# Rotary queries of layer 1: projected among the gates and kept in DRAM, instead of inside the attention

## The chip, the cores and the metric

The kernel runs on one core of one Trainium2 chip. The metric is device time in microseconds from launch to end; one execution was also taken by the hardware profiler. The engines are TensorE (PE, with its weight loads PEld), VectorE (DVE), ScalarE (ACT), GpSimd (POOL) and SyncE (SP), which issues the DMAs here.

## The reference, cut to what matters

Two layers run over 256 context tokens and 1024 latent tokens. Layer 0 is differential attention. Layer 1 is multi-head latent attention, and the change is in it:

```
proj = h @ w_in                      # -> q_a (384), kv_a (256), k_pe (64), gate (1024)
q = (rmsnorm(q_a, g_qa) @ w_qb)      # 8 heads x (128 nope + 64 rope)
q_pe = apply_rope(q[..., 128:])      # latent tokens alone; halves x1, x2 of 32:
                                     # [x1*cos - x2*sin, x1*sin + x2*cos]
s = q . [k_nope, k_pe] * 192**-0.5   # per head, 1280 keys for latents, 256 for context
o = softmax(s) @ v;  out = o * silu(gate)
```

So each of 8 heads has 128 query columns without position (qn) and 64 rotary ones (qpe); the rotary key is shared by the heads.

## The kernel before, in words

All matrix products are made in three terms of a high and a low part (`mm3`, L328 to L330: high x high, high x low, low x high), so each operand exists twice. Tokens go in 5 pairs of 128-row blocks (`NPAIR`): 4 pairs of latents, 1 pair of context.

Layer 1 has two stages that matter here. **First the projections and gates** (`l1_items`): three token items give the compressed keys, the rotary key and the compressed queries, whose normalised transposes are `m.qaT[pr]`, high and low. Then come eight `gate_item(h)`, one per head: 24 matmuls of 512 columns twice and 24 of 256 columns, into PSUM buffers of a pool of four (`pj`), each result put through a tanh on ScalarE and a product on VectorE and stored in DRAM (`gTd`). `chain` runs the items in turn; an item's `yield None` is the point at which the next item's weights are loaded, through staging buffers `wst`, of which there are three.

**Then the attention** (`l1_heads`): 8 heads x 10 blocks of queries ("units"). The order is written by hand: in turn n the scores of unit n + 2 (`l1_scores`), the values of the pair just finished (`l1_values`), the transposes of unit n, and between them "fills", generators that make the next heads' operands: `l1_kn` ("k"), `l1_qn` ("q"), `l1_v` ("v", two heads at a time, for even heads) and `l1_qpe` ("p", four heads at a time). Which fill stands where comes from `DA`, `DB`, `DC` (the start), `at(...)` and the tables `QO`, `QE`, `KS`, `VS`, `PS`. "p" of heads 0 to 3 is made in head 0, "p" of heads 4 to 7 over heads 3 and 4. Within each engine a scheduler sets the final order.

`l1_qpe` makes, for each pair, 18 matmuls with the tokens as rows, copies the result out, rotates it (six operations of 128 columns for a block, one block on VectorE, one on GpSimd; `rope_inplace`), splits it into high and low, transposes it with 8 transposes (L1219) and copies the two PSUM tiles out (L1221). The result has a head's high and low rotary columns on the 128 partitions, and the rotary part of the scores is then two matmuls, against `kpA` and `kpB`.

`weights_x` is what layer 0 uses to load weights with the two rotary halves apart: 32 first-half columns of four heads together, then the 32 second-half columns. The products made with it are transposed, and rotating them needs no shuffling inside a row.

Of the kernel before, what the change touches and what calls it, by code (L numbers as in the profile page):

```python
# [81 lines left out]
class K:  # L82
# [265 lines left out]
    def weights_x(self, W, off):  # L348


        nc, wp = self.nc, self.wp
        out = []
        for k0 in range(0, KC, 2):
            wh = self.t(wp, [P, 2, 2, P], "wh", F32R)
            wl = self.t(wp, [P, 2, 2, P], "wl", F32R)
            st = self.t(wp, [P, 2, 256], "wst", bufs=3)
            nc.sync.dma_start(st, W[:, k0:k0 + 2, off:off + 256])
# [4 lines left out]
            out += [(wh[:, :, j, :], wl[:, :, j, :]) for j in range(2)]  # L362
        return out
# [6 lines left out]
    def l0_qk_item(self, kind, hp):  # L370
# [90 lines left out]
        return lambda: self.weights_x(W, (0 if kind == "q" else 1024) + hp * 256), gen  # L461
# [742 lines left out]
    def l1_qpe(self, h, out):  # L1204

        nc, c, m, I = self.nc, self.c, self.m, self.I
        Wq = I["mla_w_qb"][0].rearrange("(kc p) n -> p kc n", p=P)
        wq = self.weights(Wq, [((h + j) * 192 + P, 64) for j in range(4)], lo_engs=self.LO[::-1] if h == 0 else None)
        yield 1
        res = out["p", h] = []  # L1210
        pend = []

        def finish(pr, qss):
            o = self.t(c.qp, [P, 4, 256], f"qpe{pr}", F32R)
            res.append(o)
            for i in range(2):
                pt = self.t(c.tp, [P, 4, P], "tp")
                for j in range(4):
                    nc.tensor.transpose(pt[:, j, :].bitcast(F32R), qss[i][:, j].rearrange("p a d -> p (a d)"),  # L1219
                                        self.identr)  # L1220
                (nc.scalar.copy if i else nc.vector.tensor_copy)(o[:, :, i * P:(i + 1) * P], pt)  # L1221
        for pr in range(NPAIR):
            ps = self.l1_ps("p")
            qt = m.qaT[pr]
            for i in range(2):
                for k in range(3):
                    self.mm3(ps[:, i, :], (qt[:, 0, k, i * P:(i + 1) * P], qt[:, 1, k, i * P:(i + 1) * P]),
                             wq[k], k == 0, k == 2)
            qss = []
            for i in range(2):  # L1230
                raw = self.t(c.rp, [P, 4, 64], "qraw", bufs=2)
                nc.scalar.copy(raw.rearrange("p a d -> p (a d)"), ps[:, i, :])
                if pr < CTXP:
                    self.rope_inplace(c.rp, raw.unsqueeze(1), 2 * pr + i, 4, nc.gpsimd if i else nc.vector, bufs=2)
                qs = self.t(c.rp, [P, 4, 2, 64], "qs", F32R, bufs=2)
                nc.vector.tensor_copy(qs[:, :, 0, :], raw)
                nc.vector.tensor_tensor(out=qs[:, :, 1, :], in0=raw, in1=f32(qs[:, :, 0, :]), op=ALU.subtract)
                qss.append(qs)
            yield 1960
            finish(pr, qss)  # L1240
            yield 470

    def l1_scores(self, u, kn, qn, qpe):
# [7 lines left out]
        qp = qpe[u.pr][:, u.h % 4, u.i * P:(u.i + 1) * P]  # L1251
# [63 lines left out]
    def l1_heads(self):  # L1315
# [78 lines left out]
    def run(self, ctx):  # L1394
# [339 lines left out]
```

## Time and profile before

| | |
|---|---|
| median of 3 runs | 2013.87 us (2013.73 to 2016.31) |
| the profiled execution, its own time | 2013.29 us |
| its span | 2011.5 us |
| gates (from 1210 us to their end at 1324.2 us) | 114.2 us |
| head 0 of the attention, with its start | 107.7 us |
| heads 1 and 2; 3 and 4; 5 and 6 | 128.2; 148.7; 129.9 us |
| DMA: q1, the SyncE queue | 222.70 MB, 35.4% of 16 engines' span |

The span runs from the first to the last instruction. A head is taken to end where the last product with its gate (L1302) starts. The busy time of an engine is the union of its instructions; the idle time of a stage is its length less that. A matmul's own duration is longer than the step to the next one, because they overlap, so prices per matmul are taken from the steps between starts.

### The profile page before, as it was taken

What the parts mean: (1) busy time and instruction counts of PE and PEld (TensorE: products, weight loads), DVE (VectorE), ACT (ScalarE), POOL (GpSimd) and SP (SyncE); (2) the same over time, 40 slices, a digit from 0 to 9 for tenths busy, and PEclk for the clock granted to TensorE, in tenths of its full rate; (3) what the DMA queues carried; (4) which work ended last, traced back from release to release, by engine and by line L of the source; (5) the groups of instructions that cost most, each with busy time, mean ns of one, the idle gap of its engine ahead of it and who ended that gap; (6) DMA issues with size and microseconds to landing.
All of it is one profiled execution on the core that took longest, in us unless ns stands there. A gap on an engine that the chain in (4) does not pass through costs nothing. (4 is left out here: it accounts for less than half of the span.)

```text
span 2011.5 us, 36299 instructions
## 1 busy us (share of the span) xinstructions
PE 1921.2 (96%) x13548; PEld 1729.7 (86%) x13548; DVE 1257.4 (63%) x2518; ACT 966.0 (48%) x2421; POOL 522.1 (26%) x740
## 2 busy tenths in 40 slices
PE   6999999999999999999989899999999999999998
PEld 5788888798988878887988898888999899998998
DVE  4634347788878777888246623157776877777413
ACT  4422124667666666677335533234444444455421
POOL 3355442213122212324243431011000110003214
PEclk9999999999999999999999999999999999999999
DMA  8545544454355453456343302210101011013412
GB/s 304 186 160 185 179 144 144 145 156 141 111 168 180 116 171 101 139 158 207 128 135 112 101 24 85 76 38 26 31 29 34 16 31 34 27 38 95 154 60 105
DMA packets 215536, 225.07 MB, mean 112 GB/s; under 512 B 24032, under 2 KB 184128, under 8 KB 215232
## 3 DMA queue, kind: packets, MB, share of 16 engines
q1 hardware_dynamic: 215200, 222.70, 35.4%
q8 instruction: 107, 1.75, 0.4%
q14 instruction: 69, 0.57, 0.1%
q10 hardware_dynamic: 160, 0.05, 0.0%
HBM read 153.14 MB, written 69.53 MB: 111 GB/s over the span
## 5 line engine op out<-in xcount | busy, mean ns | idle before, releaser
L328 PE MATMUL pj<-wh,hh 128*128 128x256 f32 (+1 forms) x1264 | 369.9, 293 | 6.6 <-DVE ptl L670 3.5
L329 PE MATMUL pj<-wl,hh 128*128 128x256 f32 (+1 forms) x1264 | 359.5, 284 | 6.0 <-DVE wl L321 3.7
L330 PE MATMUL pj<-wh,hl 128*128 128x256 f32 (+1 forms) x1264 | 359.2, 284 | 3.4 <-POOL hl L300 1.5
L321 POOL TENSOR_TENSOR wl<-wst,wh 128x512 fp32r<-128x512 f32 (+3 forms) x98 | 113.5, 1165 | 577.8 <-ACT wh L320 487.8
L328 PEld LDWEIGHTS pj<-wh,hh 128*128 128x128 f32 x1264 | 242.4, 192 | 11.6 <-DVE ptl L670 4.1
L329 PEld LDWEIGHTS pj<-wl,hh 128*128 128x128 f32 x1264 | 242.6, 192 | 8.3 <-DVE wl L321 4.1
L330 PEld LDWEIGHTS pj<-wh,hl 128*128 128x128 f32 x1264 | 242.0, 191 | 6.4 <-POOL hl L300 3.1
L330 PE MATMUL pj<-hh,wl 128*128 128x512 f32 (+1 forms) x512 | 188.5, 368 | 0.2
L328 PE MATMUL pj<-hh,wh 128*128 128x512 f32 (+1 forms) x512 | 188.3, 368 | 0.0
L329 PE MATMUL pj<-hl,wh 128*128 128x512 f32 (+1 forms) x512 | 187.8, 367 | 0.0
L601 DVE TENSOR_REDUCE mA<-S 128x1 f32<-128x1024 f32 x128 | 155.3, 1219 | 46.5 <-PE S L599 45.5
L613 ACT ACTIVATE e<-S,bias 128x1024 f32<-128x1024 f32 x128 | 142.9, 1117 | 81.4 <-DVE bias L610 81.4
L599 PE MATMUL S<-kl,q 128*128 128x512 f32 x512 | 149.1, 411 | 5.7 <-ACT e L613 5.3
L669 ACT CAST pth<-tp 128x512 fp32r<-128x512 f32 (+1 forms) x208 | 99.5, 512 | 83.1 <-PE tp L667 81.9
L669 ACT CAST pth<-pj 128x512 fp32r<-128x512 f32 (+1 forms) x192 | 98.4, 519 | 71.6 <-PE pj L667 68.8
L670 DVE TENSOR_TENSOR ptl<-tp,pth 128x512 fp32r<-128x512 f32 (+1 forms) x208 | 116.0, 580 | 15.1 <-ACT pth L669 14.3
L644 DVE SCALAR_TENSOR_TENSOR e<-e,cf,e 128x512 f32<-128x512 f32 (+1 forms) x192 | 122.5, 680 | 1.1
L670 DVE TENSOR_TENSOR ptl<-pj,pth 128x512 fp32r<-128x512 f32 (+1 forms) x192 | 112.9, 592 | 9.6 <-ACT pth L669 9.1
L320 ACT CAST wh<-wst 128x512 fp32r<-128x512 f32 (+3 forms) x140 | 78.8, 573 | 75.3 <-issue 22.0
L330 PEld LDWEIGHTS pj<-hh,wl 128*128 128x128 f32 x512 | 96.3, 188 | 20.0 <-POOL wl L361 3.0
L329 PEld LDWEIGHTS pj<-hl,wh 128*128 128x128 f32 x512 | 96.3, 188 | 16.9
L328 PEld LDWEIGHTS pj<-hh,wh 128*128 128x128 f32 x512 | 96.3, 188 | 16.4
(333 smaller groups left out, 5296.2 us busy)
## 6 DMA issues: line engine op xcount, KB each, us to landing
q<-qsd SPq DMA_DIRECT2D x320, 64.0 KB, 2.1
wst<-in_da_w_in_dram SPq DMA_DIRECT2D x64, 256.0 KB, 3.1
kl<-ksd SPq DMA_DIRECT2D x64, 192.0 KB, 3.6
wst<-in_w_out_dram SPq DMA_DIRECT2D x48, 256.0 KB, 3.0
ast<-in_w_ada_dram SPq DMA_DIRECT2D x8, 1024.0 KB, 6.4
wh<-in_w_ada_dram SPq DMA_DIRECT2D x32, 256.0 KB, 4.2
wl<-in_w_ada_dram SPq DMA_DIRECT2D x32, 256.0 KB, 5.0
vdh<-s SPq DMA_DIRECT2D x24, 256.0 KB, 2.1
```

What stands on the lines that cost most here:

```text
L320: nc.scalar.copy(wh, st)
L321: (lo_engs or [nc.gpsimd])[k0 // kb % len(lo_engs or [0])].tensor_tensor(out=wl, in0=st, in1=f32(wh), op=ALU.subtract)
L328: nc.tensor.matmul(out, a[0], b[0], start=first, stop=False)
L329: nc.tensor.matmul(out, a[0], b[1], start=False, stop=False)
L330: nc.tensor.matmul(out, a[1], b[0], start=False, stop=last)
L599: nc.tensor.matmul(S[:, so:so + 512], st(cc, o), kl[cc][:, so:so + 512], start=(o == 0), stop=(o == 1))
L601: nc.vector.reduce_max(out=mA[:, cc:cc + 1], in_=S, axis=AX.X)
L613: nc.scalar.activation(u.es[cc][:, 0:1024], A[cc], AF.Exp, bias=bias[:, cc:cc + 1], scale=0.125, accum_out=u.zA[:, cc:cc + 1])
L644: nc.vector.scalar_tensor_tensor(out=w[:, sl], in0=w[:, sl], scalar=cf, in1=e0[:, sl], op0=ALU.mult, op1=ALU.add)
L669: nc.scalar.copy(hi, tp[:, 0:cn, :])
L670: nc.vector.tensor_tensor(out=u.ptl[g][:, 0:cn, u.i * P:(u.i + 1) * P], in0=tp[:, 0:cn, :], in1=f32(hi), op=ALU.subtract)
```

## The change

The rotary queries leave the attention. Two new items `qpe_item(0)` and `qpe_item(1)` stand among the gates, behind gate 1 and behind gate 4, each for four heads. An item loads its weights with `weights_x` (now with a list of columns), and for each pair makes the 18 matmuls with the weights as the stationary side, so that the result is transposed: 128 partitions are 4 heads x 32 columns of one half, and the two halves lie side by side. The rotation of a latent pair is a ScalarE copy, two products of 512 columns with a table loaded from DRAM, a subtraction and an addition of 256 columns on VectorE; then a ScalarE cast gives the high part and VectorE the low part. Four stores put them into DRAM (`qpd`). In the attention `l1_load_p(h)` loads a head's 4 x 32 rows of 1280 columns, head 0's at the start and head h + 1's in turn 3 of head h. `l1_qpe`, its pool and its fills are gone; the pool of the loaded queries has two buffers. The transposes, two per block of four heads before, are gone with it.

```diff
-    DA, DB, DC = "kpqv", "kpqkkpp", "pvvv"
+    DA, DB, DC = "kqv", "kqkk", "vvv"
...
-    PS = (0, 1, 2, 3, 4, 5, 7, 10, 12, 13, 15)
...
-            later.add(self.split_T(tp, "tp", [qa[:, 0, :], qa[:, 1, :]], m.qaT[pr], 3), 12)
+            later.add(self.split_T(tp, "tp", [qa[:, 0, :], qa[:, 1, :]], m.qaT[pr], 3), 12, ("qa", pr))
...
+        def qpe_item(g):
...
+                for pr in range(NPAIR):
+                    if pr < CTXP:
+                        rt = table(pr)
+                    later.finish(("qa", pr))
+                    ps = self.t(pj, [P, 2, 256], "pj")
+                    qt = m.qaT[pr]
+                    for x in range(2):
+                        for k in range(3):
+                            self.mm3(ps[:, x, :], (ws[k][0][:, x, :], ws[k][1][:, x, :]), (qt[:, 0, k, :], qt[:, 1, k, :]),
+                                     k == 0, k == 2)
+                            yield 1
+                    hi, lo = (tile(1 + 2 * (pr % 2) + v, F32R) for v in range(2))
+                    r = ps
+                    if pr < CTXP:
+                        cos, sin = (rt[:, j, :].unsqueeze(1).to_broadcast([P, 2, 256]) for j in range(2))
+                        r = tile(0)
+                        t = self.t(c2.pool, [P, 2, 256], "gTh")
+                        nc.scalar.copy(r, ps)
+                        nc.vector.tensor_tensor(out=t, in0=r, in1=sin, op=ALU.mult)
+                        nc.vector.tensor_tensor(out=r, in0=r, in1=cos, op=ALU.mult)
+                        nc.vector.tensor_tensor(out=r[:, 0, :], in0=r[:, 0, :], in1=t[:, 1, :], op=ALU.subtract)
+                        nc.vector.tensor_tensor(out=r[:, 1, :], in0=r[:, 1, :], in1=t[:, 0, :], op=ALU.add)
+                    nc.scalar.copy(hi, r)
+                    nc.vector.tensor_tensor(out=lo, in0=r, in1=f32(hi), op=ALU.subtract)
+                    for j, v in enumerate((hi, lo)):
+                        for x in range(2):
+                            nc.sync.dma_start(self.qpd[g][2 * j + x][:, pr * 256:(pr + 1) * 256], f32(v)[:, x, :])
+            return lambda: self.weights_x(Wq, [((4 * g + j) * 192 + P, 64) for j in range(4)]), gen
...
+                self.l1_tok_item([(0, 256)], pj, ev_q1, lambda pr: None)] + gates[0:2] + [qpe_item(0)] + gates[2:5] + [
+                qpe_item(1)] + gates[5:] + [(self.l1_first, lambda ws: iter(()))]
...
+    def l1_load_p(self, h):
+
+        q = self.t(self.c.qp, [P, 1280], "qpe", F32R)
+        for b in range(4):
+            self.nc.sync.dma_start(f32(q)[32 * b:32 * b + 32, :], self.qpd[h // 4][b][h % 4 * 32:h % 4 * 32 + 32, :])
+        return q
...
-        at(0, 0, ("p", 0), ("v", 0), ("q", 0), ("v", 0))
-        at(0, 1, ("p", 0), ("v", 0), ("p", 0))
-        at(0, 2, ("q", 0), ("p", 0))
-        at(0, 3, ("v", 0), ("p", 0))
-        at(0, 4, ("p", 0))
+        at(0, 0, ("v", 0), ("q", 0), ("v", 0))
+        at(0, 1, ("v", 0))
+        at(0, 2, ("q", 0))
+        out["p", 0] = self.l1_load_p(0)
...
+            if n % 10 == 3 and h + 1 < H:
+                out["p", h + 1] = self.l1_load_p(h + 1)
```

Three places show how the order on the engines moves. The first is VectorE in the gates, behind the gate of head 1. Before, gate follows gate (`gT` is a gate's tanh, `gTh` its half, `wl` the low part of a weight):

```order
L1123 SCALAR_TENSOR_TENSOR gT_15415<-gT_15415,gTh_15416 128x512
L321 TENSOR_TENSOR wl_15460<-wst_15461,wh_15459 128x512
L1123 SCALAR_TENSOR_TENSOR gT_15447<-gT_15447,gTh_15448 128x256
L1123 SCALAR_TENSOR_TENSOR gT_15490<-gT_15490,gTh_15491 128x512
L1123 SCALAR_TENSOR_TENSOR gT_15522<-gT_15522,gTh_15523 128x512
```

After, the rotation stands between two gates. `qa` are the buffers of the raw, high and low queries, `wst` holds the table, `gTh` the product with the sine:

```order
L320 TENSOR_TENSOR wl_15474<-wst_15475,wh_15473 128x512
L1127 SCALAR_TENSOR_TENSOR gT_15461<-gT_15461,gTh_15462 128x256
L1164 TENSOR_TENSOR gTh_15503<-qa_3139_15502,wst_15479 128x512
L1165 TENSOR_TENSOR qa_3139_15502<-qa_3139_15502,wst_15479 128x512
L1166 TENSOR_TENSOR qa_3139_15502<-qa_3139_15502,gTh_15503 128x256
L1167 TENSOR_TENSOR qa_3139_15502<-qa_3139_15502,gTh_15503 128x256
L1169 TENSOR_TENSOR qa_3138_15501<-qa_3139_15502,qa_3137_15500 128x512
L1164 TENSOR_TENSOR gTh_15539<-qa_3145_15538,wst_15515 128x512
```

Five operations for each latent pair come in here. On ScalarE of the same place the fifth pair's cast (`qa_3160`) comes to stand behind the copies of the other pairs, two casts of gate weights (`wh`) and a gate's tanh:

```order
L1163 COPY qa_3157_15610<-pj_15589 128x512
L319 CAST wh_15656<-wst_15658 128x512
L319 CAST wh_15757<-wst_15759 128x512
L1125 ACTIVATE gT_15687<-pj_15662 128x512
L1168 CAST qa_3160_15642<-pj_15623 128x512
L1168 CAST qa_3155_15608<-qa_3157_15610 128x512
```

The PSUM buffer of the fifth pair (`pj_15623`) is read late in this row. The second place is the SyncE queue where the gates end and the attention starts. Before, behind the last stores of the gates (`gTd`):

```order
L1125 DMA gTd_3_59_118<-gT_16088 128x256
L318 DMA wst_17015<-in_mla_w_qb_dram 128x2x128
L318 DMA wst_17021<-in_mla_w_qb_dram 128x128
L1125 DMA gTd_4_60_119<-gT_16120 128x256
L1294 DMA gTl_16780<-gTd_0_21_80 128x256
```

After:

```order
L1129 DMA gTd_3_59_118<-gT_16456 128x256
L317 DMA wst_17174<-in_mla_w_kvb_dram 128x2x128
L1257 DMA qpe_16531<-qpd_0_61_120 32x1280
L1129 DMA gTd_4_60_119<-gT_16488 128x256
L1257 DMA qpe_16531<-qpd_1_62_121 32x1280
L1257 DMA qpe_16531<-qpd_2_63_122 32x1280
L1257 DMA qpe_16531<-qpd_3_64_123 32x1280
L1311 DMA gTl_16939<-gTd_0_21_80 128x256
```

Three of the four loads of head 0's rotary queries stand behind the last gate's store. The third place is VectorE in head 3, where a piece of a rotation stood among the softmax steps before (`mm`, `bias`, `Z`, `rz`: maxima, sums and their reciprocals; `qs` the split queries):

```order
L345 TENSOR_TENSOR qraw_19183<-qraw_19183,rt_19185 128x4x32
L1236 CAST qs_19192<-qraw_19183 128x4x64
L1236 CAST qs_19204<-qraw_19195 128x4x64
L1237 TENSOR_TENSOR qs_19192<-qraw_19183,qs_19192 128x4x64
L1282 TENSOR_TENSOR Z_19137<-Z_19137 128x1
L1237 TENSOR_TENSOR qs_19204<-qraw_19195,qs_19204 128x4x64
L1284 RECIPROCAL rz_19161<-Z_19137 128x1
```

After, the same softmax steps without it:

```order
L1293 TENSOR_SCALAR bias_19237<-mm_19236 128x1
L674 TENSOR_TENSOR ptl_3823_19213<-tp_19272,pth_3820_19210 128x4x128
L1287 TENSOR_REDUCE mm_19286<-S_19289 128x1
L1299 TENSOR_TENSOR Z_19238<-Z_19238 128x1
L1289 TENSOR_REDUCE mm_19286<-tp_19285 128x1
L1301 RECIPROCAL rz_19262<-Z_19238 128x1
```

The sum `Z` and its reciprocal follow the maxima, with no rotary row ahead of them.

## Rows read from the trace of the kernel before

**Rows 1.** The page's table of busy time, share of the span, instructions.

```profile
PE 1921.2 (96%) x13548; PEld 1729.7 (86%) x13548; DVE 1257.4 (63%) x2518; ACT 966.0 (48%) x2421; POOL 522.1 (26%) x740
```

**Rows 2.** Busy time by stage: gates; head 0; heads 1-2; 3-4; 5-6.

```profile
core 0: us, PE busy (x) PEld busy (x) DVE busy (x) ACT busy (x) POOL busy (x), PEclk, DMA share, GB/s
1210.00:1324.20 114.20, 114.11 (x592) 96.33 (x591) 28.50 (x39) 34.20 (x72) 11.45 (x12) 1.00 0.28 80
1324.20:1431.94 107.74, 102.84 (x756) 94.52 (x755) 76.30 (x185) 49.34 (x121) 18.31 (x33) 1.00 0.11 30
1431.94:1560.11 128.17, 127.32 (x914) 116.85 (x914) 91.81 (x216) 64.11 (x155) 5.45 (x7) 1.00 0.10 29
1560.11:1708.79 148.68, 144.04 (x1048) 131.26 (x1047) 111.09 (x267) 71.14 (x172) 20.37 (x33) 1.00 0.09 28
1708.79:1838.67 129.88, 128.15 (x917) 117.19 (x917) 94.80 (x221) 68.70 (x167) 12.83 (x15) 1.00 0.15 49
```

**Rows 3.** Timeline of VectorE: start, duration; last products of heads 0, 2, 4, 6.

```profile
1431.94 0.40 DVE L1302 TENSOR_TENSOR yT<-tp,gTl 128x256 f32<-128x256 f32 x1
...
1560.11 0.42 DVE L1302 TENSOR_TENSOR yT<-tp,gTl 128x256 f32<-128x256 f32 x1
...
1708.79 0.41 DVE L1302 TENSOR_TENSOR yT<-tp,gTl 128x256 f32<-128x256 f32 x1
...
1838.67 0.42 DVE L1302 TENSOR_TENSOR yT<-tp,gTl 128x256 f32<-128x256 f32 x1 [0.26 <-PE tp L667]
```

**Rows 4.** Chain of waits in head 0: start, time on the chain.

```profile
1380.43 0.63 PE tp L1219 x8
```

**Rows 5.** Timeline of TensorE: gate matmuls of 512, of 256; rotary matmuls in the attention.

```profile
1212.34 0.39 PE L328 MATMUL pj<-hh,wh 128*128 128x512 f32 x1
...
1212.80 0.40 PE L330 MATMUL pj<-hh,wl 128*128 128x512 f32 x1
...
1321.73 0.28 PE L328 MATMUL pj<-hh,wh 128*128 128x256 f32 x1
...
1324.10 0.28 PE L330 MATMUL pj<-hh,wl 128*128 128x256 f32 x1
...
1327.76 0.28 PE L328 MATMUL tp<-qaT,wh 128*128 128x256 f32 x1
...
1329.77 0.28 PE L330 MATMUL tp<-qaT,wl 128*128 128x256 f32 x1
```

**Rows 6.** Timeline of VectorE, ScalarE and GpSimd in the first gates.

```profile
1213.17 0.62 DVE L1036 SCALAR_TENSOR_TENSOR qa<-qa,rs,gq 128x384 f32<-128x384 f32 x1 [0.95 <-POOL rs L254]
...
1214.44 1.29 POOL L321 TENSOR_TENSOR wl<-wst,wh 128x512 fp32r<-128x512 f32 x1
...
1214.51 1.64 DVE L1036 SCALAR_TENSOR_TENSOR qa<-qa,rs,gq 128x384 f32<-128x384 f32 x1 [0.38 <-POOL rs L254]
...
1216.79 0.59 ACT L1025 CAST qaT<-tp 128x512 fp32r<-128x512 f32 x1 [3.28 <-PE tp L1023]
1217.40 0.69 DVE L1026 TENSOR_TENSOR qaT<-tp,qaT 128x512 fp32r<-128x512 f32 x1 [1.26 <-ACT qaT L1025]
...
1218.37 0.42 DVE L1026 TENSOR_TENSOR qaT<-tp,qaT 128x256 fp32r<-128x256 f32 x1 [0.27 <-ACT qaT L1025]
```

**Rows 7.** Line 424, a rotary product of layer 0: ns minimum/median/maximum, first and last start.

```profile
L424 DVE TENSOR_TENSOR r<-r,ropeT x16: 691/691/694, 89.0 to 278.1; 128x512 f32<-128x512 f32 x16
```

**Rows 8.** Timeline of the SyncE queue at the end of the gates.

```profile
1324.30 1.20 SPq L318 DMA_DIRECT2D wst<-in_mla_w_qb_dram  x2
1325.64 0.33 SPq L1125 DMA_DIRECT2D gTd<-gT  x1
```

**Rows 9.** DMA issues by name: count, KB each, median us to landing.

```profile
kl<-ksd SPq DMA_DIRECT2D x64, 192.0 KB, 3.6
...
wst<-in_mla_w_in_dram SPq DMA_DIRECT2D x24, 256.0 KB, 2.8
```

**Rows 10.** Groups by line: count, busy us, mean ns of one, idle before, releasers.

```profile
L1219 PE MATMUL tp<-identr,qs 128*128 128x128 f32 x80 | 9.2, 250 | 2.1 <-DVE qs L1237 0.9 <-DVE qn L1178 0.9 <-DVE knl L1159 0.2
```

More of the change, by code (lines that the diff above doesn't have):

```diff
@@ L346, in rope_inplace, with weights_x @@
         eng.tensor_tensor(out=x2, in0=x2, in1=b[:, 1], op=ALU.add)
-    def weights_x(self, W, off):
+    def weights_x(self, W, cols):
         nc, wp = self.nc, self.wp
+        nk = W.shape[1]
         out = []
[L353 to L357, printed above, removed]
+        for k0 in range(0, nk, 2):
+            kn = min(2, nk - k0)
+            wh = self.t(wp, [P, 2, kn, P], "wh", F32R)
+            wl = self.t(wp, [P, 2, kn, P], "wl", F32R)
+            st = self.t(wp, [P, kn, 256], "wst", bufs=3)
+            o = 0
+            for off, w in cols:
+                nc.sync.dma_start(st[:, :, o:o + w], W[:, k0:k0 + kn, off:off + w])
+                o += w
             sv = st.rearrange("p k (g x d) -> p (k g) x d", g=4, x=2)
@@ L361, in weights_x @@
             nc.gpsimd.tensor_tensor(out=vl, in0=sv, in1=f32(vh), op=ALU.subtract)
-            out += [(wh[:, :, j, :], wl[:, :, j, :]) for j in range(2)]
+            out += [(wh[:, :, j, :], wl[:, :, j, :]) for j in range(kn)]
         return out
@@ L460, in gen @@
                 yield 360
-        return lambda: self.weights_x(W, (0 if kind == "q" else 1024) + hp * 256), gen
+        return lambda: self.weights_x(W, [((0 if kind == "q" else 1024) + hp * 256, 256)]), gen
     def l0_tok_item(self, kind, hp, each=None):
@@ L1126, in gate_item, with gen, table @@
             return lambda: self.weights(W, [(704 + h * P, P)], kb=4, lo_engs=self.LO), gen
+        Wq = I["mla_w_qb"][0].rearrange("(kc p) n -> p kc n", p=P)
+        def qpe_item(g):
+            def gen(ws):
+                yield None
+                tile = lambda j, dt=F32: self.t(c2.pool, [P, 2, 384], f"qa{j}", dt).rearrange("p a b -> p (a b)")[
+                    :, 0:512].rearrange("p (a b) -> p a b", a=2)
+                def table(pr):
+                    rt = self.t(self.wp, [P, 2, 256], "wst", bufs=3)
+                    nc.sync.dma_start(rt, I["ropeT"][:, :, pr * 256:(pr + 1) * 256])
+                    return rt
+                for pr in range(NPAIR):
[26 more added lines that the diff above has]
+            return lambda: self.weights_x(Wq, [((4 * g + j) * 192 + P, 64) for j in range(4)]), gen
@@ L1128, in l1_items @@
+        gates = [gate_item(h) for h in range(H)]
         return [self.l1_tok_item([(384, 256)], pj, ev_kva, lambda pr: later.finish(("h", pr))),
                 self.l1_tok_item([(256, 128), (640, 64)], pj, ev_q2, lambda pr: None),
-                self.l1_tok_item([(0, 256)], pj, ev_q1, lambda pr: None)] + [gate_item(h) for h in range(H)] + [(self.l1_first, lambda ws: iter(()))]
+                self.l1_tok_item([(0, 256)], pj, ev_q1, lambda pr: None)] + gates[0:2] + [qpe_item(0)] + gates[2:5] + [
+                qpe_item(1)] + gates[5:] + [(self.l1_first, lambda ws: iter(()))]
@@ L1202, in l1_v @@
             yield 1310
[L1204 to L1241, printed above, removed]
+    def l1_load_p(self, h):
[3 more added lines that the diff above has]
+        return q
     def l1_scores(self, u, kn, qn, qpe):
@@ L1250, in l1_scores @@
         qh, ql = qn[u.pr][:, 0, u.i * P:(u.i + 1) * P], qn[u.pr][:, 1, u.i * P:(u.i + 1) * P]
-        qp = qpe[u.pr][:, u.h % 4, u.i * P:(u.i + 1) * P]
+        qp = qpe[:, u.pr * 256 + u.i * P:u.pr * 256 + (u.i + 1) * P]
         e = self.t(c.ep, [P, 1280], "e")
@@ L1305, in l1_gen @@
     def l1_gen(self, kind, h):
-        return {"k": self.l1_kn, "q": self.l1_qn, "v": self.l1_v, "p": self.l1_qpe}[kind](h, self.out)
+        return {"k": self.l1_kn, "q": self.l1_qn, "v": self.l1_v}[kind](h, self.out)
     def l1_first(self):
@@ L1328, in scores @@
                 u = units[n]
-                self.l1_scores(u, out["k", u.h], out["q", u.h], out["p", u.h - u.h % 4])
+                self.l1_scores(u, out["k", u.h], out["q", u.h], out["p", u.h])
         fills = {n: [] for n in range(len(units) + 2)}
@@ L1345, in l1_heads @@
                     at(h, max(j, 0 if h else 4), (kind, g))
-        for j in self.PS:
-            at(3, j, ("p", 4))
         for it in self.DB:
@@ L1354, in l1_heads @@
         scores(1)
-        self.pd = "pq"
+        self.pd = "q"
         for n, u in enumerate(units):
@@ L1404, in run @@
         self.gTd = [[self.t(dp, [P, 256], f"gTd{h}_{p}") for p in range(NPAIR)] for h in range(H)]
+        self.qpd = [[self.t(dp, [P, 1280], f"qpd{g}_{b}") for b in range(4)] for g in range(2)]
         self.yTd = [[self.t(dp, [P, 256], f"yTd{h}_{p}") for p in range(NPAIR)] for h in range(H)]
@@ L1639, in run @@
             c.qn = pool(s1, "qn")
-            c.qp = pool(s1, "qp1")
+            c.qp = pool(s1, "qp1", 2)
             c.vp = pool(s1, "vp1")
@@ L1644, in run @@
             c.st = pool(s1, "st1", 2)
-            c.rp = pool(s1, "rp1", 1)
             c.pj = pool(s1, "pj4", self.DP, space=PSUM)
@@ L1648, in run @@
             c.tp, c.ttag = pool(s1, "tps1", self.DT, space=PSUM), "tp"
-            self.pd = "kqvp"
+            self.pd = "kqv"
             self.l1_heads()
```

## The prediction

> **What bounds the kernel now.** I read the page's busy table first [rows 1]. The reader is to see that TensorE is busy for 96% of the span, but this share is an average, so the next view is the one that asks what each stage waits for: busy time by stage, cut at the two places that the change touches and at the ends of heads [rows 2]. In the 114.2 us of the gates TensorE idles 0.1 us: each matmul put there costs its full time, and each wait of another engine there is free as long as it stays shorter than the work in front of it. In the attention TensorE idles 4.9 us in head 0 (107.74 less 102.84), 0.9 us in heads 1 and 2 together, 4.6 us in heads 3 and 4, 1.7 us in heads 5 and 6. Heads 0, 3 and 4 are those that make rotary queries (four heads' worth in head 0, the other four spread over heads 3 and 4), and the VectorE column rises with them: 111.1 us against 91.8 and 94.8 us for the pairs of heads beside them. So the rotary queries cost matmul time, and beyond it waits on VectorE.
>
> The third view gives this a price without any model: the time at which the last product of a head leaves [rows 3]. Heads 1 and 2 take 1560.11 - 1431.94 = 128.17 us, heads 3 and 4 take 148.68 us, heads 5 and 6 take 129.88 us. Each pair holds one odd and one even head with the same fills, except for the rotary queries of heads 4 to 7, and the matmul counts of [rows 2] differ by 131 to 134 where the rotary step has 130. So that step costs 148.68 - 129.03 = 19.65 us where it stands (18.8 to 20.5 by either neighbour).
>
> **The change part by part.**
>
> *Products.* Both kernels make 2 groups x 5 pairs x 18 = 180 matmuls of 256 columns. In the attention 18 of them start over 2.01 us, 0.118 us each; in the last gate 21 start over 2.37 us, 0.1185 us each [rows 5]. Out of the attention go 180 x 0.118 = 21.3 us, into the gates come 21.3 us, which nothing there can hide. Net: nothing.
>
> *Transposes.* 80 transposes of the split queries fall away. In the chain of waits eight of them take 0.63 us, 0.079 us each [rows 4]: 80 x 0.079 = 6.3 us, 3.15 us a group, all on the engine that sets the end.
>
> *Waits in heads 3 and 4.* Of the 19.65 us, 90 x 0.118 = 10.6 us only moves, which leaves 9.0 us (8.2 to 9.9) as gain. 3.15 us of it are transposes; the other 5.9 us are waits, and the cause is the 16 to 19 us of VectorE work (rotation, splitting, copying out) that goes with the step. What is late next there is TensorE itself, as in heads 1 and 2.
>
> *Head 0.* It has no sibling to subtract. The transposes give 3.15 us. Its idle time is 4.9 us against 0.4 us for an ordinary head; some of that is the start of the attention, where nothing is in flight yet. In heads 3 and 4 an extra idle time of about 3.4 us went with 5.9 us of wait, so the waits here lie between 0 (all of it is the start) and 4.5 x 5.9 / 3.4 = 7.8 us. I take 4.0, near the middle, since VectorE also has the rotary work here. Head 0: 7.15 us, between 3.15 and 11.
>
> *The rotation among the gates.* Per pair of context blocks it is now a ScalarE copy, four VectorE operations (two of 512, two of 256 columns), a ScalarE cast and a VectorE subtraction. By the nearest rows [rows 6, 7]: 0.59 + 2 x 0.69 + 2 x 0.42 + 0.59 + 0.69 = 4.1 us, about 4.2 us with the handing over, and the pairs follow each other, because they share one buffer for the raw queries. TensorE makes a pair in 18 x 0.118 = 2.1 us, so the rotation falls behind, and what matters is when the four PSUM buffers come free. The first that can hurt is that of the fifth pair, wanted again by the second gate after the step: 10.6 us for the step and 48 x 0.23 + 24 x 0.118 = 13.9 us for the gate in between [rows 5], that is 24.5 us after the step began. On ScalarE the fifth pair's cast stands behind four raw copies, three of the casts, a gate's tanh and the cast of a gate's weights that are loaded into the buffer of the fourth pair's table. Adding up: 2.1 + 3 x 4.2 + 0.6 = 15.3 us to the fourth copy, then 2.5 us of VectorE work up to the last reader of that table, 2.8 us for the load [rows 9], three ScalarE operations and the subtraction, 2.5 us: about 23.2 us. It just fits, with 1.3 us to spare, so the cost lies between 0 and, with a load twice as slow, 2 x 1.5 us. I take 1 us for both groups and 4 us as the bad end.
>
> GpSimd is the risk in this. Next to a 1.29 us subtraction on GpSimd a VectorE operation with two SBUF inputs took 1.64 us instead of 0.62 us [rows 6]. The Trainium skill, "GPSIMD Engine Reference", section "1. Specifications", says that its SBUF interfaces are shared with VectorE and contend with instructions that have two SBUF inputs, which all five VectorE steps of a pair are. By that rule alone each of them would be open to it; by the rows only those that fall beside one of the two such subtractions of an item, which adds 1 to 2 us and uses up about the spare time. It is the second rival below.
>
> *Queues.* The SyncE queue gets 40 stores, 8 table loads and 32 loads of 160 KB. The loads of heads 1 to 7 are issued a head ahead and are hidden by the whole head. Head 0's cannot be early: three of its four parts stand in the queue behind the last gate's store, which waits for VectorE. From the end of the gates (1324.10 + 0.12, [rows 5]) that store issues after 1.4 us [rows 8]; three issues of up to 0.6 us and 3.6 us until a load of like shape lands [rows 8, 9] make 7.2 us. TensorE first reads it behind 79 matmuls of 256, 4 of 512 and 3 of 256 columns, 10.6 us after the gates. Cost 0; were that cover gone, up to 3.6 us. The rotary weights are cast by the same engines as before, only earlier: 0.
>
> **Sum.** -9.0 (heads 3, 4) - 7.15 (head 0) + 1 (gates) = -15.15 us. Against the profiled execution (2013.29 us, its span 2011.5) that is 1998.1; the median of the runs shown is 0.6 us higher, so 1998.7, which I round to 1999. The ends: -9.9 - 11 = -20.9 us gives 1993, -8.2 - 3.15 + 4 = -7.4 us gives 2006.
>
> **Rivals.** *A, the waits come back.* VectorE was late because of the softmax steps, and without the 180 matmuls there is less to fill TensorE while it waits. Then only the transposes are gained: -6.3 + 1, 2008.5. For it: the chain of a head is long, and part of the idle time in head 0 is the start. Against it: heads 1, 2, 5, 6 have no such matmuls and idle less, not more.
>
> *B, slower: the rotation holds up the gates.* The place is the fifth pair's PSUM buffer. Each microsecond that a pair's chain grows arrives there four times, in each of two groups, less the 1.3 us to spare. The gain is used up, and the 0.2% with it, from (15.15 + 1 + 4) / 2 = 10 us a group, (10 + 1.3) / 4 = 2.8 us a pair, 7.0 instead of 4.2 us. If every VectorE step of a pair were slowed as the one row shows, by 1.0 us, the chain is 9.2 us and the loss 2 x (4 x 5 - 1.3) = 37 us: 2036. For it: the rows of contention. Against it: GpSimd works only 11.5 of the 114.2 us of the gates [rows 2].
>
> *C, the queries arrive late in head 0*, as priced above: 2002. For it: a SyncE queue that serves in order. Against it: 3.4 us to spare.
>
> *D, a transpose holds TensorE for all of its duration.* One lasts 0.250 us in the mean [rows 10]; 80 x (0.250 - 0.079) = 13.7 us more gain, 1985. Against it stands the chain, where eight took 0.63 us. The Trainium skill, "TensorE: Matmul & The Clock Gate", section "Part 4: PE-mode transpose", gives about 275 ns for one inside a kernel, an estimate of 80 x 0.275 = 22 us where the sum has 6.3; the trace agrees with it as a duration and not as a rate.
>
> **How the numbers follow.** Forecast 0.66; A 0.17 (a third of it gains under 4 us); B 0.09 (slower 0.05, no difference 0.03, faster 0.01); C 0.07; D 0.01. About 0.2%, 4 us, is what a measurement of this kernel can tell from no change. Faster: 0.66 + 0.07 + 0.01 + 0.12 + 0.01 = 0.87; same 0.05 + 0.03 = 0.08; slower 0.05. The range 1993 to 2008 leaves out most of B, half of A, D, and the forecast's own low end: about 0.2.
>
> **What the profile will show.** Right: the gates about 136 us long with TensorE idle under 2 us; heads 3 and 4 at 128 to 130 us with VectorE near 93 us and TensorE idle under 2 us; head 0 near 90 us (107.7 - 10.6 - 7.2); no wait for the loaded queries. Wrong: TensorE waiting in the gates for the cast or the subtraction of the fifth pair (B), a wait for the load of the queries at the head of the attention (C), or heads 3 and 4 that idle longer than heads 1 and 2 (A).

## The result, and the profile after

The changed kernel takes 1996.67 us in the median (1993.42 to 1997.65, 5 runs) against 2013.87 us before: a ratio of 0.9909, 95% interval [0.9896, 0.9922], or 18.3 us less (15.7 to 20.9). I had forecast 1999.0 us, 14.9 us less. The profiled execution took 1997.65 us, its span 1995.8 us. The page's busy table, to be held against [rows 1]:

```profile
PE 1911.7 (96%) x13468; PEld 1721.9 (86%) x13468; DVE 1248.4 (63%) x2461; ACT 963.9 (48%) x2409; POOL 498.9 (25%) x693
```

Exactly 80 matmul instructions are gone, the transposes. The shares have not moved, though the kernel is faster: they are averages, as in the view before. What moved is seen by stage. The busy time of each engine in the gates, head 0, heads 1-2, 3-4, 5-6 and 7 of the changed kernel, the answer to [rows 2]:

```profile
core 0: us, PE busy (x) PEld busy (x) DVE busy (x) ACT busy (x) POOL busy (x), PEclk, DMA share, GB/s
1214.31:1349.09 134.78, 134.69 (x767) 116.89 (x765) 53.62 (x81) 46.21 (x93) 14.92 (x16) 1.00 0.42 127
1349.09:1438.82 89.73, 87.78 (x626) 79.89 (x625) 59.56 (x136) 42.62 (x104) 5.85 (x8) 1.00 0.19 54
1438.82:1566.27 127.45, 126.97 (x914) 116.83 (x914) 91.50 (x215) 63.89 (x155) 5.56 (x7) 1.00 0.14 39
1566.27:1694.03 127.76, 127.12 (x916) 116.99 (x915) 91.59 (x217) 63.78 (x155) 5.55 (x7) 1.00 0.14 40
1694.03:1823.89 129.86, 128.06 (x919) 117.31 (x918) 94.82 (x222) 68.25 (x167) 12.79 (x15) 1.00 0.18 54
1823.89:1874.24 50.35, 45.70 (x321) 40.20 (x320) 34.95 (x79) 26.82 (x67) 11.59 (x15) 1.00 0.22 66
```

The gates are read here from their first matmul (1214.31 us), not from a round time as in [rows 2]. The same cut of the kernel before has these two rows, for the gates and for head 7:

```profile
1210.72:1324.21 113.49, 113.40 (x586) 95.62 (x585) 28.21 (x39) 33.48 (x71) 10.73 (x12) 1.00 0.28 80
...
1838.67:1889.96 51.29, 46.69 (x321) 41.53 (x321) 35.48 (x78) 26.76 (x67) 11.51 (x15) 0.97 0.22 65
```

| stage | before, us | after, us | moved | forecast |
|---|---|---|---|---|
| gates | 113.5 | 134.8 | +21.3 | +22.3 |
| head 0 | 107.7 | 89.7 | -18.0 | -17.75 |
| heads 1, 2 | 128.2 | 127.5 | -0.7 | 0 |
| heads 3, 4 | 148.7 | 127.8 | -20.9 | -19.65 |
| heads 5, 6 | 129.9 | 129.9 | 0.0 | 0 |
| head 7 | 51.3 | 50.4 | -0.9 | 0 |
| sum | 679.2 | 659.9 | -19.3 | -15.1 |

The rows show three things. TensorE idles 0.1 us in the gates, as before: the rotation, 25 us more of VectorE, is hidden entirely. Heads 3 and 4 now have the length, the matmul count and the VectorE time of heads 1 and 2: they have become an ordinary pair. And the work ahead of the gates, which the change does not touch, ended at 1210.72 us in the profile of before and at 1214.31 us in that of after. In the ten further profiles below it ended between 1209.7 and 1214.0 us, with either form of the kernel, so this difference of 3.6 us is scatter of single executions; it is why the spans differ by 15.7 us and the stages by 19.3.

### The profile page after: what moved, and what is told of

Read it like the earlier page. It is cut to its first block, busy times and chain, and to the rows that moved or that the text cites. A ratio compares the mean times of both kernels' runs of the same rounds, so it can differ in the third digit from the quotient of the medians.

```text
span 1995.8 us, 36154 instructions
## 1 busy us (share of the span) xinstructions
PE 1911.7 (96%) x13468; PEld 1721.9 (86%) x13468; DVE 1248.4 (63%) x2461; ACT 963.9 (48%) x2409; POOL 498.9 (25%) x693
## 4 chain that ended last, share of the span: by engine, by line
PE 43%; DVE 5%; POOL 3%; ACT 2%; issue 2%; DMA 2%; SPq 0%; POOLq 0%; ACTq 0%; DVEq 0%
PE pj L327 7%; PE pj L329 7%; PE pj L328 7%; PE tp L671 3%; PE tp L327 3%; PE tp L328 3%; PE tp L329 3%; PE S L1280 1%; PE S L1281 1%; PE S L1278 1%; PE S L1279 1%; PE S L1277 1%; PE S L603 1%; DVE ptl L674 1%; DMA yst<-yTd 1%
## 5 line engine op out<-in xcount | busy, mean ns | idle before, releaser
L329 PEld LDWEIGHTS pj<-hh,wl 128*128 128x128 f32 x512 | 96.3, 188 | 20.9 <-POOL wl L365 3.9
L603 PEld LDWEIGHTS S<-kl,q 128*128 128x128 f32 x512 | 88.8, 192 | 25.1 <-ACT e L617 8.1
```

Source lines behind the costliest of these rows:

```text
L329: nc.tensor.matmul(out, a[1], b[0], start=False, stop=last)
L603: nc.tensor.matmul(S[:, so:so + 512], st(cc, o), kl[cc][:, so:so + 512], start=(o == 0), stop=(o == 1))
```

## The experiments

The sum came out right, but it rested on a split that no row showed: 3.15 us of transposes and 5.9 us of waits in heads 3 and 4. My theory (theory 1 below) was that the waits are VectorE's load, and that the transposes' time comes on top. The rival (theory 2) was that the transposes, queued on TensorE behind the splitting, are what waits.

**Without the rotation.**

```diff
-                if pr < CTXP:
-                    self.rope_inplace(c.rp, raw.unsqueeze(1), 2 * pr + i, 4, nc.gpsimd if i else nc.vector, bufs=2)
```

> The kernel before, with the rotation of the rotary queries left out (they stay unrotated); the matmuls, the splitting, the transposes and the copies stay. Theory 1, the waits in heads 0, 3 and 4 come from VectorE's own load: its work in heads 3 and 4 falls by about a third of the 17.8 us that the step has there, so heads 3 and 4 fall from 148.7 us to 143 to 147 us, head 0 from 107.7 to 105 to 107 us, the time by 3 to 8 us to 2006 to 2011 us. Theory 2, the waits come from the transposes, which stand in TensorE's queue behind the splitting: the rotation is only a part of the chain ahead of them, heads 3 and 4 stay within 1.5 us of 148.7 and the time within 3 us of 2013.9.

Head 0 and heads 3 and 4 of this kernel, same columns as above:

```profile
1327.26:1429.25 101.99, 101.70 (x756) 94.30 (x755) 68.45 (x160) 49.26 (x121) 6.64 (x9) 1.00 0.11 31
1557.40:1701.44 144.04, 142.85 (x1048) 131.16 (x1047) 102.14 (x242) 70.49 (x172) 7.41 (x9) 1.00 0.10 28
```

Head 0 loses 5.7 us, heads 3 and 4 lose 4.6 us; the ratio to before is 0.994 [0.9918, 0.9963]. The transposes all still stand (1048 matmuls, as before) and TensorE idles 1.2 us instead of 4.6 us. What TensorE waits for in heads 3 and 4 of the kernel before (who waits, for whom: us in total, times, longest):

```profile
PE tp L328 <- DVE ptl L670: 2.9, 3, 1.5
PE tp L1260 <- DVE ptl L670: 1.2, 1, 1.2
```

Here `ptl` are the low parts of the probabilities, a softmax step on VectorE. None of the waits there ends with the split queries that the transposes (L1219) read, and without the rotation this is the longest one left:

```profile
PE tp L1219 <- DVE qpe L1221: 0.8, 1, 0.8
```

So theory 2, which had heads 3 and 4 within 1.5 us of 148.7, falls for them; in head 0 the transposes do wait, for 2.1 of its 4.9 us of idle time [rows 10]. Head 0 gave a little more than theory 1 allowed, and so did the time, 2004.93 us where 2006 to 2011 was expected.

**Without the transposes.** Copies from SBUF take the place of the copies from PSUM. It ran twice:

```diff
-                pt = self.t(c.tp, [P, 4, P], "tp")
-                for j in range(4):
-                    nc.tensor.transpose(pt[:, j, :].bitcast(F32R), qss[i][:, j].rearrange("p a d -> p (a d)"),
-                                        self.identr)
-                (nc.scalar.copy if i else nc.vector.tensor_copy)(o[:, :, i * P:(i + 1) * P], pt)
+                (nc.scalar.copy if i else nc.vector.tensor_copy)(o[:, :, i * P:(i + 1) * P],
+                                                                 f32(qss[i]).rearrange("p j a d -> p j (a d)"))
```

> The kernel before, with the 80 transposes of the rotary queries left out: the two copies of 512 columns for each pair read the split queries in SBUF instead of PSUM, so the scores get wrong rotary queries, and VectorE and ScalarE have the same number of operations. Theory 1, the waits are VectorE's load: only the transposes' own 0.079 us each is gained, 3.15 us a group: heads 3 and 4 at 145.5 us, head 0 at 104.6 us, time 2007.6 us. Theory 2, the transposes in TensorE's queue are what waits: their waits go too, heads 3 and 4 at 138.8 to 141 us, head 0 at 100 to 102 us, time 1996 to 2001 us. If a transpose held TensorE for its 0.25 us (the rival D of the prediction), 10 us a group: heads 3 and 4 at 138.7 us with TensorE busy 10 us less, not 3 us.

> The same kernel as the earlier run without transposes (copies from SBUF in their place, wrong rotary queries), once more, because in its profile the granted clock was 0.98 over heads 3 and 4 where the kernel before had 1.00. If the transposes stood in time that TensorE had to wait anyway for VectorE: heads 3 and 4 at 147 to 149 us, head 0 at 104.2 us. If the clock hid a gain of 40 x 0.079 us: heads 3 and 4 at 145.5 us.

The first run gave heads 3 and 4 of 150.2 us at a granted clock of 0.98, longer than before, and a ratio of 0.998 [0.9963, 0.9997]. The second, head 0 and heads 3 and 4:

```profile
1326.53:1430.85 104.32, 98.61 (x714) 90.80 (x713) 75.55 (x183) 48.85 (x121) 18.58 (x33) 1.00 0.11 31
1559.01:1707.71 148.70, 141.61 (x1008) 129.09 (x1007) 108.87 (x266) 70.43 (x172) 20.33 (x33) 0.99 0.09 28
```

With 40 transposes fewer heads 3 and 4 are as long as before (148.7 us), and TensorE idles 148.70 - 141.61 = 7.1 us instead of 4.6 us. Its longest waits there, and a stretch of 6 us at a lower clock:

```profile
PE tp L328 <- DVE ptl L670: 3.7, 3, 1.7
PE tp L1257 <- DVE ptl L670: 1.3, 1, 1.3
PE tp L667 <- ACT e L1276: 1.1, 2, 0.9
```

```profile
1588.00:1594.00 6.00, 6.00 (x38) 6.00 (x39) 3.78 (x11) 2.82 (x7) 0.00 (x0) 0.72 0.00 0
```

The low parts of the probabilities are waited for 5.0 us instead of 4.1, and ScalarE's exponentials (`e`) for 1.1 us: of what the transposes gave up, 2.5 us was waited instead. The lower clock can hide at most 6.00 x (1 - 0.72) = 1.7 us, so the 40 transposes alone are worth 0 to 1.7 us here, not 3.15. In head 0 there was a gain of 3.4 us. Over the whole kernel the ratio is 0.9982 [0.997, 0.9994], where theory 1 wanted 2007.6 us, 6.3 us less than before, and the run gave 2010.67 us beside 2013.35 us. So theory 1 is wrong in its second half for heads 3 and 4: the two prices do not add.

**Without both.**

> The kernel before without rotation and without transposes (both left out, wrong queries). Without the rotation alone heads 3 and 4 took 144.05 us and head 0 101.99 us, with TensorE idle 1.2 and 0.3 us. If the transposes cost their 0.079 us each once VectorE is no longer late: heads 3 and 4 at 140.9 us, head 0 at 98.8 us, time 6 us under that without rotation, about 1998 to 1999 us. If they cost nothing in either case: 144 and 102 us, time about 2005 us.

```profile
1323.16:1423.77 100.61, 98.50 (x716) 90.57 (x715) 68.27 (x161) 49.15 (x121) 6.80 (x9) 1.00 0.11 32
1552.00:1692.82 140.82, 138.88 (x1008) 127.68 (x1007) 100.30 (x242) 70.11 (x172) 7.36 (x9) 1.00 0.10 29
```

Heads 3 and 4 fall from 144.04 to 140.82 us, (144.04 - 140.82) / 40 = 0.080 us a transpose, the price of the chain [rows 4]. So a transpose costs its step where TensorE is the bound, and little or nothing (the 0 to 1.7 us above for all 40) where TensorE waits for VectorE anyway. The Trainium skill, "TensorE: Matmul & The Clock Gate", section "Part 4: PE-mode transpose", gives about 275 ns for one in a kernel. Here such a figure is a duration, 0.250 us in [rows 10], and taking 40 of them out moved the end by 0.080 us each. In head 0 the fall is 1.4 us where 3.15 was expected: TensorE's busy time fell by 3.2 us, but its idle time rose from 0.3 to 2.1 us. The time is 1997.95 us, ratio 0.9917 [0.9894, 0.994].

**The matmuls alone.** Rotation, splitting and transposes are out; ScalarE copies each product twice:

```diff
+                for a in range(2):
+                    nc.scalar.copy(o[:, :, i * P + 64 * a:i * P + 64 * (a + 1)], qss[i])
```

> The kernel before, with rotation, splitting and transposes of the rotary queries left out: the 180 matmuls stay in the attention, and ScalarE copies the products from PSUM twice into the place of the queries (wrong queries). If the step cost 10.6 us a group for its matmuls and the rest for what hangs behind them, heads 3 and 4 take 128 + 10.6 = 138.4 us, head 0 89.7 + 10.6 = 100.3 us, and the time is that of the changed kernel, 1996.7 us, within 3 us. If matmuls in the attention cost more there than in the gates (rival), heads 3 and 4 stay over 141 us.

```profile
1326.39:1426.24 99.85, 98.12 (x716) 90.73 (x715) 60.91 (x136) 48.76 (x126) 6.31 (x9) 1.00 0.11 32
1554.38:1695.24 140.86, 139.00 (x1008) 127.83 (x1007) 93.12 (x217) 69.99 (x177) 7.14 (x9) 1.00 0.10 29
```

VectorE has 7 us less to do in heads 3 and 4 than in the run before (93.1 against 100.3 us) and the length is the same: once the rotation is gone VectorE is no longer late, and splitting is free. The time, 1996.89 us, is that of the changed kernel. But 140.9 is not the 138.4 us that both theories wanted: 90 matmuls in the attention cost 140.86 - 127.76 = 13.1 us, not 10.6. Of the 2.5 us TensorE's idle time explains 1.2 (1.86 against 0.64 us); the rest I have not traced. In head 0 the products cost 99.85 - 89.73 = 10.1 us.

**All of the rotation on GpSimd.** This takes the rotation's load from VectorE and makes the way from product to split queries longer.

```diff
-                    self.rope_inplace(c.rp, raw.unsqueeze(1), 2 * pr + i, 4, nc.gpsimd if i else nc.vector, bufs=2)
+                    self.rope_inplace(c.rp, raw.unsqueeze(1), 2 * pr + i, 4, nc.gpsimd, bufs=2)
```

> The kernel before with the rotation of both blocks of a pair on GpSimd instead of one on VectorE. By the rows a block costs VectorE about 2.2 us and GpSimd about 3.7 us. If the waits are the load of VectorE: it is relieved of 8.9 us a group, heads 3 and 4 at 144 to 146 us, head 0 at 102 to 105 us, time 2005 to 2009 us. If they are the length of the chain from a pair's matmuls to its transposes: the chain grows by about 4 us a pair, heads 3 and 4 stay at 148.7 us or grow to 152 us, time 2013 to 2020 us.

It is slower, by more than either expectation allowed: 2031.77 us, ratio 1.0088 [1.007, 1.0107]. VectorE has less to do than before (104.4 us in heads 3 and 4 against 111.1), and the pair takes 157.6 us, of which some 3 us (an estimate, 2% of the pair) go with a granted clock of 0.98. The timeline of VectorE in head 3, and a little later TensorE (start, duration, operation, idle time ahead and what ended it):

```profile
1578.62 0.54 DVE L1236 CAST qs<-qraw 128x256 fp32r<-128x256 f32 x1 [2.71 <-POOL qraw L345]
...
1581.32 0.29 DVE L1236 CAST qs<-qraw 128x256 fp32r<-128x256 f32 x1 [1.57 <-POOL qraw L345]
1581.65 0.43 DVE L1237 TENSOR_TENSOR qs<-qraw,qs 128x256 fp32r<-128x256 f32 x1
1581.99 0.15 DVE L1282 TENSOR_TENSOR Z<-Z 128x1 f32<-128x1 f32 x1
1582.18 0.16 DVE L1284 RECIPROCAL rz<-Z 128x1 f32<-128x1 f32 x1
1582.26 0.67 DVE L670 TENSOR_TENSOR ptl<-tp,pth 128x512 fp32r<-128x512 f32 x1
```

```profile
1582.99 0.38 PE L1260 MATMUL tp<-knl,qn 128*128 128x256 f32 x1 [3.53 <-DVE ptl L670]
```

VectorE stands still for GpSimd at the cast of the split queries, and behind it in its queue stand the sums, the reciprocal and the low parts of the probabilities (L670), which TensorE waits for 3.5 us. This shows what "VectorE's load" means: the rotary step holds VectorE's queue ahead of the softmax steps, by working or by waiting, and taking work away while leaving a wait at the same place made it worse. In heads 3 and 4 VectorE waits 13.1 us for GpSimd at that cast, where its own share of the rotation was 111.1 - 102.1 = 9.0 us of work (with and without the rotation). These 4.1 us and the 3 us of the clock leave 1.8 of the 8.9 us more that are not traced.

**The two groups apart.** Heads 0 to 3 changed, heads 4 to 7 as before:

```diff
-... gates[0:2] + [qpe_item(0)] + gates[2:5] + [qpe_item(1)] + gates[5:] ...
+... gates[0:2] + [qpe_item(0)] + gates[2:] ...
...
+        for j in (0, 1, 2, 3, 4, 5, 7, 10, 12, 13, 15):
+            at(3, j, ("p", 4))
```

> The changed kernel for heads 0 to 3 alone; heads 4 to 7 get their rotary queries in heads 3 and 4 as before. The loaded queries go into five tiles by twenty loads at the start, so as to need no more SBUF. If the parts are separate: gates 113.5 + 10.6 = 124.1 us, head 0 at 89.7 us (up to 3 us more if the twenty loads come late), heads 3 and 4 as before at 148.7 us; time 2013.9 - 18.0 + 10.6 - 0.7 = 2005.8 us. If the waits of heads 3 and 4 were owed to something that the change moved elsewhere (the memory layout, the stage before), heads 3 and 4 fall too, below 146 us, and the time below 2003 us.

```profile
1213.99:1338.14 124.15, 124.06 (x677) 106.25 (x675) 41.05 (x60) 39.91 (x82) 13.27 (x14) 1.00 0.35 105
1338.14:1427.69 89.55, 87.64 (x626) 79.93 (x625) 59.48 (x136) 42.55 (x104) 5.85 (x8) 1.00 0.24 62
1555.86:1704.45 148.59, 144.00 (x1048) 131.22 (x1047) 111.08 (x266) 71.04 (x172) 20.35 (x33) 1.00 0.09 28
```

Gates, head 0, heads 3 and 4: 124.2, 89.6 and 148.6 us where 124.1, 89.7 and 148.7 were expected. So the halves of the change are separate: the first has the price of the table above, and heads 3 and 4 keep their old length without the second. The ratio is 0.9952 [0.9929, 0.9974], 2007.11 us.

**The rotation made longer.** This is the mechanism of rival B.

```diff
-                        nc.vector.tensor_tensor(out=t, in0=r, in1=sin, op=ALU.mult)
+                        for _ in range(5):
+                            nc.vector.tensor_tensor(out=t, in0=r, in1=sin, op=ALU.mult)
```

> The changed kernel, with the first product of each latent pair's rotation made five times instead of once, which lengthens a pair's chain among the gates by 4 x 0.73 = 2.9 us. In the profile of the changed kernel the fifth pair's PSUM buffer is read for the last time 21.3 us after the step began and wanted 24.7 us after it, 3.4 us to spare. Rival B's mechanism (the chain holds that buffer): the read moves to 32.9 us, TensorE waits 4 x 2.9 - 3.4 = 8.2 us in each of the two steps, gates 134.8 + 16.4 = 151 us, time 2013 us. If the rotation is hidden whatever its length (another buffer, another order), gates stay at 134.8 to 136 us and the time within 2 us of 1996.7.

The gates take 148.7 us, 13.9 more (151 expected), the time is 2009.19 us (2013 expected), ratio to before 0.9982 [0.9973, 0.9991]. The three matmuls of the first step at which TensorE waits, from its timeline:

```profile
1260.22 0.50 PE L327 MATMUL pj<-hh,wh 128*128 128x512 f32 x1 [0.96 <-ACT qa L1163]
1268.46 0.38 PE L327 MATMUL pj<-hh,wh 128*128 128x256 f32 x1 [2.38 <-ACT qa L1163]
1273.61 0.47 PE L327 MATMUL pj<-hh,wh 128*128 128x512 f32 x1 [2.04 <-DVE qa L1170]
```

The last is the place that I had named, the fifth pair's buffer, held by its subtraction (L1170 in this kernel). The two ahead of it wait for the copies of the third and fourth pair, which I had not named. The idle time is 9.4 us in all, yet the gates are 13.9 us longer. Stretches of 6 us around the third wait, and one of the second step, show part of the rest:

```profile
1267.60:1273.60 6.00, 3.10 (x24) 2.93 (x25) 5.27 (x8) 2.71 (x5) 1.84 (x1) 1.00 0.65 185
1273.60:1279.60 6.00, 6.00 (x19) 4.81 (x20) 4.25 (x7) 2.64 (x5) 1.28 (x1) 0.72 0.69 210
1279.60:1285.60 6.00, 6.00 (x27) 4.82 (x27) 1.12 (x2) 1.17 (x3) 0.00 (x0) 1.00 0.77 237
...
1327.60:1333.60 6.00, 4.62 (x24) 4.42 (x24) 5.22 (x7) 2.80 (x6) 1.77 (x1) 0.72 0.67 193
```

Behind the waits the mean granted clock of a stretch is 0.72, so part of it ran at 1.2 GHz: 19 matmuls in 6 us where the next stretch has 27. TensorE's busy time in the gates grows by 139.3 - 134.7 = 4.6 us for the same 767 matmuls. The two stretches at 0.72 account for at most 2 x 1.7 = 3.4 us of that; the rest I have not traced.

**The steps back to back.**

```diff
-... gates[0:2] + [qpe_item(0)] + gates[2:5] + [qpe_item(1)] + gates[5:] ...
+... gates[0:2] + [qpe_item(0), qpe_item(1)] + gates[2:] ...
```

> The changed kernel, with the second rotary step directly behind the first instead of three gates later. Mechanism of rival B, with four PSUM buffers, 2.13 us of TensorE for a pair and 4.3 to 5.4 us of rotation: the third and fourth pair of the second step wait about 2 us each for a buffer and the first tile of the next gate 1.4 us: TensorE waits 5.7 us (4 to 12 with the weight buffers, which the tables share), gates at 139 to 147 us, time 2001 to 2009 us. If the gates between the steps are not what covers the rotation, gates stay at 134.8 us and the time at 1996.7 us.

The gates take 141.5 us, 6.7 more: 4.2 us of waits, 1.86, 1.88 and 0.44 us at the three places expected (5.7 us expected), and again a lower clock behind the first two (0.82 and 0.90 in two neighbouring stretches of 6 us). The time is 2000.87 us, ratio to before 0.9939 [0.9926, 0.9953]. So the gates in between are what hides the rotation.

**Filling head 7.** TensorE still idles 4.65 us in head 7 of the changed kernel. This was the one place found where a version could beat both.

```diff
+                    if g == H - 1 and kind == "q" and n > 1:
+                        at(g, (0, 0, 1, 5)[n], (kind, g))
```

> The changed kernel, with the last two pieces of the queries without position of head 7 (pairs 2 and 3, and pair 4: 54 matmuls, 6.4 us) made in head 7 instead of head 6. Head 7 has no such work now and TensorE idles 4.65 us in it, 1.6 us in head 6. If the idle time is there because nothing fills it: head 6 falls by 6 to 7 us, head 7 grows by 3 to 4.5 us, the time falls by 2 to 3.5 us to about 1994 us. If the idle time is a chain that the moved work, with its VectorE steps, lengthens: no gain, within 1 us, or a loss.

```profile
1754.54:1819.56 65.02, 64.42 (x462) 58.98 (x462) 47.93 (x110) 33.33 (x79) 3.30 (x3) 1.00 0.12 37
1819.56:1875.86 56.30, 52.81 (x378) 47.33 (x377) 35.94 (x87) 32.66 (x83) 19.18 (x25) 1.00 0.31 94
```

Heads 6 and 7 take 65.02 + 56.30 = 121.3 us against 70.2 + 50.35 = 120.6 us. TensorE's idle time fell from 6.2 to 4.1 us and its busy time rose by 2.9 us, for a reason that I have not traced: less idle on paper and nothing gained. The time is 1998.12 us, within the scatter of 1996.67. No version here beats the changed kernel.

## Why the prediction was right

**Products.** The gates grew by 21.3 us for 180 x 0.118 us, to the tenth. Out of the attention went more than the 21.3 us of the prediction: by the run with the matmuls alone 10.1 us in head 0 and 13.1 us in heads 3 and 4, together 23.2. So "Net: nothing" was 1.9 us too careful.

**Gates, +1 us forecast, 0 measured.** The step begins on TensorE at 1243.56 us and the fifth pair's buffer is wanted again 24.7 us later (24.5 forecast). On VectorE two rows show the state of the chain:

```profile
1255.84 1.78 DVE L1165 TENSOR_TENSOR qa<-qa,wst 128x512 f32<-128x512 f32 x1
...
1264.21 0.68 DVE L1169 TENSOR_TENSOR qa<-pj,qa 128x512 fp32r<-128x512 f32 x1
```

The second is the last reader, done 1264.89 - 1243.56 = 21.3 us after the start where I had 23.2: 3.4 us to spare instead of 1.3. The first is the contention that I feared, and it came: the product that takes 0.69 us elsewhere took 1.78 us beside this subtraction on GpSimd.

```profile
1255.78 1.29 POOL L320 TENSOR_TENSOR wl<-wst,wh 128x512 fp32r<-128x512 f32 x1 [24.19 <-ACT wh L319]
```

GpSimd ended at 1257.07 us and VectorE 0.55 us behind it, less than a whole product: as if it had waited out the other engine. The Trainium skill, "Trainium Architecture — The Big Picture", section "What this means for kernel authors", calls the shared port an exclusive lock and not a split of bandwidth; this row agrees. It happened twice in the first step, 2 x 1.1 us, a little over the 1 to 2 us that I had set against the spare time. The spare time held even so, because a term of the sum was not on the path. I had the fifth pair's cast wait for gate weights that are loaded into the buffer of the fourth pair's table, 2.5 + 2.8 us. On ScalarE two casts of gate weights, then a gate's tanh and the fifth pair's cast ran one behind the other without a wait:

```profile
1260.36 1.15 ACT L319 CAST wh<-wst 128x512 fp32r<-128x512 f32 x2
...
1261.90 0.59 ACT L1168 CAST qa<-pj 128x512 fp32r<-128x512 f32 x1
```

Rival B is a true mechanism with the wrong size here. With 2.9 us more a pair (the run with five products) its formula takes away 2 x (4 x 2.9 - 1.3) = 20.6 us, more than the whole gain; the gates grew by 13.9 us, of which 9.4 us are waits, and the kernel stayed faster than before. The formula had too little spare time, and it left out the lower clock that came behind the waits.

**Head 0.** -18.0 us against -17.75; that it came so close is luck. The 7.15 us beyond the products were guessed from a wide bound (3.15 to 11) as 4.0 of waits and 3.15 of transposes. The runs give 5.7 us for the rotation alone, 3.4 us for the transposes alone and 7.1 us for both: the sum was right, the parts overlap.

**Heads 3 and 4.** -20.9 us against -19.65, and here a step failed though the number held. The total was read from sibling heads and so did not need the parts. Its split, "3.15 us of it are transposes; the other 5.9 us are waits", is wrong in its second half. The rotation alone gave 4.6 us, of which 3.45 are idle time of TensorE, as the idle times of [rows 2] already had it (4.6 us against 1.3 in a sibling pair). The transposes gave 3.2 us on top of it, but only 0 to 1.7 us by themselves. That is 7.9 us; the last 2.5 us went with the matmuls, 13.1 us where the prediction had 10.6. The 1.2 us of my miss in the total come from the siblings: I averaged heads 1-2 and 5-6, and the latter are 1.7 us longer for a reason of their own (129.9 us before and after); by heads 1-2 alone the price is 148.68 - 128.17 = 20.5 us.

**Rival A** had it the wrong way round. It kept the transposes as the one safe gain and let the waits come back. There the transposes were the part that hardly counted by itself, and the waits did not come back: TensorE idles 0.64 us in heads 3 and 4.

**Rival C**, the queue. The SyncE queue at the end of the gates, to be held against [rows 8]:

```profile
1349.66 0.44 SPq L1257 DMA_DIRECT2D qpe<-qpd  x1
1350.70 0.33 SPq L1129 DMA_DIRECT2D gTd<-gT  x1
1351.08 2.37 SPq L1257 DMA_DIRECT2D qpe<-qpd  x3
```

Three loads did stand behind the last gate's store. They were issued by 1353.45 us and such a load lands after 3.1 us in the median, at about 1356.6 us, 7.5 us after the gates (7.2 forecast). TensorE first uses the queries here:

```profile
1359.83 0.46 PE L1280 MATMUL S<-kpA,qpe 128*128 128x512 f32 x1
```

That is 10.7 us after the gates, without a wait (10.6 forecast). **Rival D**, that a transpose holds TensorE for its whole duration, is refuted: taking one out gave 0.080 us, not 0.250.

**Outside the sum** lie 0.7 us in heads 1 and 2 and 0.9 us in head 7. The 0.7 us do not come from the step in head 0: with heads 0 to 3 changed alone, heads 1 and 2 took 128.17 us, as before; the cause is open. In head 7 the clock was 0.97 before and 1.00 after, and it took between 48.1 and 51.3 us in the kernels in which its code is the same, so I count this as scatter.

## What to carry to other kernels

Price a step by the stage that has it less a sibling stage that has not; such a difference held here although its causes had been split wrongly, and prices of parts taken out of it singly need not add up. Where an engine waits for another, its own work in front of that wait can be nearly free, as the transposes were in heads 3 and 4, and removing it shows little until the other engine is on time. Before moving work between engines, look at what stands behind it in the queue: a wait at that place holds up the queue as the work did.

## What was not expected of the hardware

Waits of 1 to 2.4 us on TensorE, a few microseconds apart, were followed by a stretch with a mean granted clock of 0.72, in both steps of the kernel with the longer rotation, and of 0.82 and 0.90 in the one with the steps back to back. In the former 9.4 us of waiting went with 13.9 us more of gates.

Such a fall is not tied to the waits alone. Head 0 is the same in the changed kernel, in the one with the longer rotation and in the one that fills head 7, and TensorE waits the same 0.9, 0.7 and 0.2 us in it. It took 89.7 us in the first and 91.25 us in the other two:

```profile
1362.26:1453.51 91.25, 89.30 (x626) 81.37 (x625) 59.56 (x135) 42.58 (x104) 5.84 (x8) 0.98 0.19 53
1348.48:1439.73 91.25, 89.31 (x626) 81.43 (x625) 59.58 (x136) 42.59 (x104) 5.86 (x8) 0.98 0.19 53
```

Their granted clock is 0.98 where the changed kernel has 1.00, and the 1.5 us are what that cost. A difference of this size between two profiles is to be held against the clock before it is given to the change.
